# Rotary embedding on one core: longer VectorE operations and stores by even and odd partitions

## Chip, cores and metric

The kernel runs on one core of a Trainium2 chip. The metric is the device time of one execution in microseconds. The times given are medians over several runs; the profile is of one execution, whose own time is given beside it.

## What is computed

The reference applies a rotary position embedding. `x` is float32 of 16 x 512 x 1024; its last dimension is 16 heads of 64. `cos` and `sin` are 512 x 32 and depend on the position in the sequence alone.

```python
x = x.reshape(batch, seq, num_heads, head_dim)
x1, x2 = x[..., :half_dim], x[..., half_dim:]
cos = cos[None, :, None, :]
sin = sin[None, :, None, :]
rotated = np.concatenate([x1 * cos - x2 * sin, x1 * sin + x2 * cos], axis=-1)
```

33.6 MB come in and 33.6 MB go out.

## The kernel before, in words

**Slabs.** The work is cut into eight slabs of 4 MB, 0 to 7. A slab lies on all 128 partitions with eight rows of 1024 elements (8192 float32, 32 KB) on each. Two slabs share a batch of 16 rows a partition, so in DRAM the 32 KB runs of neighbouring partitions of one slab start 64 KB apart (`rows`, L67).

**Room.** One tile, `room` (L58), holds six slots of 32 KB a partition, 0 to 5. The same bytes seen as bf16 are `halves` (L59): twelve half places of 8192 elements, where halves 2k and 2k+1 are the lower and the upper half of slot k. Three tables say where a slab lies: `land[s]` (L62) is the slot that slab s is loaded into, `home[s]` (L63) the half place that holds it as bf16, and `leave[s]` (L64) the slot that it is widened into and stored from.

**Steps of a slab.** A load (L82, issued on SP's queue) brings float32 into its slot. `cast` (L153, ScalarE, L154) writes it as bf16 to its home. `turn` (L162, VectorE) rotates it in place, in two parts of 4096 elements, each of three operations: the slab with the halves of each head swapped, times the sin table, into `turned_part` (in the tile `spare`, L168); the slab times the cos table, in place (L168); the sum of both, in place (L171). `spread` (L157, ScalarE, L158) widens the result to float32 in the slot it leaves from, and a store (L86, SP's queue) writes it out.

**Tables.** The cos and sin rows are loaded by two small DMAs on ScalarE's queue (L105), cast by GpSimd (L137), spread over the partitions by eight matmuls with a selection matrix (L145) and copied to bf16 by VectorE (L150), one table for even and one for odd slabs.

**Order.** From L174 on, the order on ScalarE, VectorE and SP is the order in which the calls are written. SP's queue takes the loads 0 to 5, then 6, then 7 in two pieces, then the stores 0 to 7 (store 1 in two pieces of 4096 elements). A DMA on SP waits until what it needs is done, and those written after it wait behind it. Load 6 goes into a slot that an earlier slab's cast has left, load 7 likewise. `first` (L193), store 0, is made to wait for the larger piece of load 7 (`gate`, L188). The waits between engines and DMAs are put in by the language's tracking of which parts of a tile each instruction reads and writes; they count up semaphores, one for each engine, and eight for the DMAs in turn.

Of the kernel before, what the change touches and what calls it, by code (L numbers as in the profile page):

```python
# [9 lines left out]
@with_exitstack  # L10
def kernel(
    ctx: ExitStack,
    tc: tile.TileContext,
    x: bass.AP,
    cos: bass.AP,
    sin: bass.AP,
    num_heads: int,
    out: bass.AP,
):
    nc = tc.nc  # L20
    P = nc.NUM_PARTITIONS

    batch, seq, dim = x.shape
    nh = num_heads
    hd = dim // nh
    half = hd // 2
    bf16 = mybir.dt.bfloat16
    f32 = mybir.dt.float32

    nb = 2  # L30
    slots = 6
    TAIL = 2
    nslabs = batch // nb
    G = 2
    rpp = nb * seq // P
    W = rpp * dim
    SP = seq // rpp
    TW = rpp * half

    out_flat = out.rearrange("b s h d -> b s (h d)")  # L40

    singles = ctx.enter_context(tc.tile_pool(name="singles", bufs=1))
    psum = ctx.enter_context(tc.tile_pool(
        name="psum", bufs=1, space=bass.MemoryType.PSUM))


    def dram(t, s, k):
        return bass.AP(tensor=t.tensor,
                       offset=t.offset + s // G * (G * nb * seq * dim) + s % G * W,
                       ap=[[G * W, P], [1, k * W]])  # L50


    def view(t, offset, *dims):
        return dataclasses.replace(t, offset=t.offset + offset,
                                   ap=[t.ap[0], *[list(d) for d in dims]])


    room = singles.tile([P, slots * W], f32, tag="room")  # L58
    halves = room.bitcast(bf16)  # L59


    land = (0, 1, 2, 3, 4, 5, 2, 3)  # L62
    home = (0, 1, 2, 3, 8, 9, 0, 1)  # L63
    leave = (5, 2, 5, 1, 2, 4, 5, 0)  # L64


    def rows(t, s, r, n):  # L67
        return bass.AP(
            tensor=t.tensor,
            offset=t.offset + s // G * (G * nb * seq * dim) + s % G * W + r * dim,  # L70
            ap=[[G * W, P], [1, n * dim]])


    def wide(slot, r, n):
        return view(room, slot * W + r * dim, (1, n * dim))


    def thin(s, r, n):
        return view(halves, home[s] * W + r * dim, (1, n * dim))


    def load(s, r, n):  # L82
        return nc.sync.dma_start(out=wide(land[s], r, n), in_=rows(x, s, r, n))


    def store(s, r, n):  # L86
        return nc.sync.dma_start(out=rows(out_flat, s, r, n), in_=wide(leave[s], r, n))

    TR = 32
    TQ = seq // TR // rpp
    TC = seq * half // TR
    spare = singles.tile([P, rpp // 2 * dim // 2], f32, tag="spare")
    turned_part = spare.bitcast(bf16)
    raw = view(spare, 0, (1, TC))
    nc.vector.memset(raw, 0.0)  # L97


    def load_tables(queue):  # L100
        for i, src in enumerate((cos, sin)):
            to = dataclasses.replace(
                raw, offset=raw.offset + i * raw.ap[0][0],
                ap=[[P // TR * raw.ap[0][0], TR], [1, TC]])
            queue.dma_start(out=to, in_=bass.AP(  # L105
                tensor=src.tensor, offset=src.offset, ap=[[TC, TR], [1, TC]]))


    load(0, 0, rpp)
    load_tables(nc.scalar)  # L110
    for s in range(1, slots):
        load(s, 0, rpp)

    GP = SP // G
    GT = G // TQ
    pick = singles.tile([P, 3 * GT * P], bf16, tag="pick")
    nc.gpsimd.memset(pick, 0.0)  # L119


    def selection(g, h):
        return pick[:, (g * GT + h // TQ) * P:(g * GT + h // TQ + 1) * P]


    for g in range(3):
        for h in range(0, G, TQ):
            part = view(selection(g, h), 0, (GP, P // GP), (1, GP))
            nc.gpsimd.affine_select(  # L129
                out=part, in_=part, compare_op=mybir.AluOpType.not_equal,  # L130
                fill=-1.0 if g == 2 else 1.0,
                base=-(1 if g else 0) - h // TQ * (P // TR),
                pattern=[[0, P // GP], [-(G // TQ) * (P // TR), GP]],
                channel_multiplier=1)

    raw_b = singles.tile([P, TC], bf16, tag="raw_b")
    nc.gpsimd.tensor_copy(out=raw_b, in_=raw)  # L137

    tab = {}


    def table(h):
        acc = psum.tile([P, 2 * rpp * hd], f32, tag=f"acc{h}")
        for g, at in ((0, 0), (0, half), (2, rpp * hd), (1, rpp * hd + half)):
            nc.tensor.matmul(  # L145
                view(acc, at, (hd, rpp), (1, half)), selection(g, h),
                view(raw_b, h % TQ * TW, (half, rpp), (1, half)),
                start=True, stop=True)
        tab[h] = singles.tile([P, 2 * rpp * hd], bf16, tag=f"tab{h}", name="tab")
        nc.vector.tensor_copy(out=tab[h], in_=acc)  # L150


    def cast(s, r=0, n=rpp):  # L153
        nc.scalar.copy(out=thin(s, r, n), in_=wide(land[s], r, n))  # L154


    def spread(s, r=0, n=rpp):  # L157
        nc.scalar.copy(out=wide(leave[s], r, n), in_=thin(s, r, n))  # L158
        return store(s, r, n)


    def turn(s):  # L162
        n = rpp // 2
        for r in (0, n):
            low = thin(s, r, n)
            flip = view(low, half, (hd, n * nh), (-half, 2), (1, half))
            for out_, in_, a in ((turned_part, flip, rpp * hd), (low, low, 0)):
                nc.vector.tensor_mul(  # L168
                    out=out_, in0=in_,
                    in1=view(tab[s % G], a + r * hd, (hd, n), (0, nh), (1, hd)))  # L170
            nc.vector.tensor_add(out=low, in0=low, in1=turned_part)  # L171


    with tc.manual_schedule(engines={  # L174
            mybir.EngineType.Activation, mybir.EngineType.DVE, mybir.EngineType.SP}):
        n = rpp // 2
        cast(0, 0, n)
        cast(0, n, n)
        for h in range(G):
            table(h)  # L180
        turn(0)
        cast(1)
        turn(1)
        cast(2)
        load(6, 0, rpp)
        turn(2)
        cast(3)
        gate = load(7, 0, rpp - TAIL)  # L188
        load(7, rpp - TAIL, TAIL)
        turn(3)  # L190
        cast(4)
        cast(5)
        first = spread(0)  # L193
        tc.add_manual_dep(
            first.ins, gate.ins.name,
            mybir.DependencyInfo(mybir.DependencyClass.Sync,
                                 mybir.DependencyReason.DATA),
            reason="behind the loads")
        turn(4)
        cast(6)  # L200
        spread(1, 0, n)
        spread(1, n, n)
        turn(5)
        spread(2)
        spread(3)
        spread(4)
        turn(6)
        cast(7)
        turn(7)
        spread(5)  # L210
        spread(6)
        spread(7)


# [33 lines left out]
```

## Time and profile before

| | us |
|---|---|
| median of 3 runs (161.9 to 162.2) | 162.07 |
| the profiled execution | 162.36 |
| its span, first to last instruction | 160.6 |
| VectorE busy (51 instructions) | 112.8 |
| ScalarE busy (19 instructions) | 113.5 |
| cast of 128x8192, f32 to bf16, mean | 7.018 |
| spread of 128x8192, bf16 to f32, mean | 7.017 |
| VectorE product or sum of 128x4096 bf16, mean | 2.292 |
| a 4 MB store, issue to landing, median | 14.8 |

The profile's page gives busy time of each engine, its busy tenths in 40 slices of the span, the DMA queues (q1 is SP's), and the chain of work that ended last. SP's own waits say what each DMA on SP's queue was held by before it was issued. The timeline lists instructions in order: start, duration, engine, line, operation, output and inputs, and in brackets the idle time before it with what ended it. The trace also keeps, for each DMA, the moment at which each of the 16 DMA engines reported its part landed; "landing" means the last of the 16 unless said otherwise. DMA work overlaps everything else; transfers of one queue are worked off in the order of issue, and one issued while others are under way waits behind them.

### The profile page before, as it was taken

The page shows a single profiled execution, that of the slowest core. Times are in us where ns is not written, and L with a number is a line of the kernel's source. Part 1 is how long each engine was busy: PE and PEld are TensorE (multiplying, and loading weights), DVE is VectorE, ACT ScalarE, POOL GpSimd, SP SyncE. Part 2 cuts the span into 40 slices and gives each one's busy share as a digit, 9 for nine tenths or more (in the row PEclk, how much of TensorE's full clock was granted, in tenths as well). Part 3 has the DMA queues.
Part 4 walks back from the last instruction along what each step waited for, and adds up shares of the span by engine and source line. Part 5 has one row for each costly group of instructions (what it writes and reads, how often), then busy time and mean ns, then how long its engine had stood idle before and what let it go on. Part 6 is the DMA issues. An engine that isn't in the chain of part 4 may idle for free.

```text
span 160.6 us, 195 instructions
## 1 busy us (share of the span) xinstructions
PE 1.9 (1%) x8; PEld 1.1 (1%) x8; DVE 112.8 (70%) x51; ACT 113.5 (71%) x19; POOL 2.1 (1%) x9
## 2 busy tenths in 40 slices
PE   0004000000000000000000000000000000000000
PEld 0002000000000000000000000000000000000000
DVE  1002999999999999999999999999739990000000
ACT  3006949488493966999999799999999999800000
POOL 3001000000000000000000000000000000000000
DMA  7999999999999999999899999999999999999993
GB/s 261 408 408 408 506 392 392 498 416 392 490 424 392 473 441 392 457 392 465 375 506 416 392 441 473 392 433 482 392 433 475 392 416 498 392 392 514 400 392 139
DMA packets 2689, 67.25 MB, mean 419 GB/s; under 512 B 320, under 2 KB 320, under 8 KB 384
## 3 DMA queue, kind: packets, MB, share of 16 engines
q1 hardware_dynamic: 2592, 67.11, 97.4%
q10 hardware_dynamic: 96, 0.13, 0.2%
q14 instruction: 1, 0.01, 0.0%
HBM read 33.69 MB, written 33.55 MB: 419 GB/s over the span
## 4 chain that ended last, share of the span: by engine, by line
DVE 62%; ACT 13%; DMA 7%; issue 3%; PE 1%; POOLq 0%; ACTq 0%; DVEq 0%
DVE room L171 20%; DVE room L168 20%; DVE spare L168 20%; ACT room L158 9%; DMA spare<-in_sin_dram 7%; ACT room L154 4%; DVE tab L150 1%; PE acc L145 1%; POOLq L243 0%; ACTq L105 0%; DVE spare L97 0%; DVEq L168 0%; POOLq L137 0%; ACTq L158 0%
## 5 line engine op out<-in xcount | busy, mean ns | idle before, releaser
L154 ACT CAST room<-room 128x8192 bf16<-128x8192 f32 (+1 forms) x9 | 56.3, 6259 | 22.6 <-DMA room<-in_x_dram 22.5
L158 ACT CAST room<-room 128x8192 f32<-128x8192 bf16 (+1 forms) x9 | 56.0, 6258 | 1.3 <-DMA out_dram<-room 1.0
L168 DVE TENSOR_TENSOR spare<-room,tab 128x4096 bf16<-128x4096 bf16 x16 | 36.7, 2292 | 4.5 <-ACT room L154 3.6
L168 DVE TENSOR_TENSOR room<-room,tab 128x4096 bf16<-128x4096 bf16 x16 | 36.7, 2292 | 0.5
L171 DVE TENSOR_TENSOR room<-room,spare 128x4096 bf16<-128x4096 bf16 x16 | 36.7, 2292 | 0.5
L150 DVE CAST tab<-acc 128x1024 bf16<-128x1024 f32 x2 | 2.4, 1220 | 13.6 <-PE acc L145 13.6
L154 ACT ACT_TABLE_LOAD x1 | 1.3, 1283 | 2.6 <-issue 2.6
L145 PE MATMUL acc<-raw_b,pick 128*128 128x256 bf16 x8 | 1.9, 416 | 13.9 <-POOL raw_b L137 13.9
L145 PEld LDWEIGHTS <-pick 128*128 128x128 bf16 x8 | 1.1, 139 | 14.2 <-issue 12.2
L97 DVE MEMSET spare<- 128x512 f32 x1 | 0.5, 485 | 0.9 <-PEq L229 0.9
L129 POOL TENSOR_SCALAR_AFFINE_SELECT pick<-pick 128x128 bf16<-128x128 bf16 x3 | 0.8, 308 | 0.1
L137 POOL CAST raw_b<-spare 128x512 bf16<-128x512 f32 x1 | 0.6, 610 | 11.2 <-DMA spare<-in_sin_dram 11.2
L119 POOL MEMSET pick<- 128x384 bf16 x1 | 0.4, 417 | 0.3 <-POOLq L229 0.3
L229 POOL MEMSET const-bfloat16-1.0<- 128x1 bf16 x1 | 0.1, 101 | 0.0
L229 POOL MEMSET const-uint8-127<- 128x1 uint8 x1 | 0.1, 101 | 0.0
L229 POOL MEMSET const-float32-0.0<- 128x1 f32 x1 | 0.1, 98 | 0.2 <-issue 0.2
L229 POOL MEMSET const-float32-1.0<- 128x1 f32 x1 | 0.1, 98 | 0.0
## 6 DMA issues: line engine op xcount, KB each, us to landing
room<-in_x_dram SPq DMA_DIRECT2D x7, 4096.0 KB, 31.7
out_dram<-room SPq DMA_DIRECT2D x7, 4096.0 KB, 14.8
out_dram<-room SPq DMA_DIRECT2D x2, 2048.0 KB, 9.9
room<-in_x_dram SPq DMA_DIRECT2D x1, 3072.0 KB, 29.4
room<-in_x_dram SPq DMA_DIRECT2D x1, 1024.0 KB, 31.5
spare<-in_cos_dram ACTq DMA_DIRECT2D x1, 64.0 KB, 7.9
spare<-in_sin_dram ACTq DMA_DIRECT2D x1, 64.0 KB, 11.1
```

What stands on the lines that cost most here:

```text
L97: nc.vector.memset(raw, 0.0)
L119: nc.gpsimd.memset(pick, 0.0)
L129: nc.gpsimd.affine_select(out=part, in_=part, compare_op=mybir.AluOpType.not_equal, fill=-1.0 if g == 2 else 1.0, base=-(1 if g else 0) - ...
L137: nc.gpsimd.tensor_copy(out=raw_b, in_=raw)
L145: nc.tensor.matmul(view(acc, at, (hd, rpp), (1, half)), selection(g, h), view(raw_b, h % TQ * TW, (half, rpp), (1, half)), start=True, sto ...
L150: nc.vector.tensor_copy(out=tab[h], in_=acc)
L154: nc.scalar.copy(out=thin(s, r, n), in_=wide(land[s], r, n))
L158: nc.scalar.copy(out=wide(leave[s], r, n), in_=thin(s, r, n))
L168: nc.vector.tensor_mul(out=out_, in0=in_, in1=view(tab[s % G], a + r * hd, (hd, n), (0, nh), (1, hd)))
L171: nc.vector.tensor_add(out=low, in0=low, in1=turned_part)
L229: nc = _bacc.Bacc("TRN2", target_bir_lowering=False, num_devices=1)
```

## The change

Five parts.

- Slabs 0, 1, 2, 5 and 7 (`aside`) are rotated in three operations of 8192 elements instead of six of 4096. The products with sin go into a half place that is free at the time instead of `turned_part`. Slabs 3, 4 and 6 are rotated as before.
- Slabs 6 and 7 change landing slots (6 into slot 3, 7 into slot 2), and slabs 1 and 4 leave from slot 3 instead of slot 2.
- Load 5 is issued after turn(0) is written, not among the first loads, since the sin products of slab 0 lie in slot 5.
- Slab 0 is cast in one operation instead of two, cast(3) is written ahead of load 6 and turn(2), and turn(3) behind cast(5).
- The stores of slabs 2 to 5 are two DMAs each (`twice`): the even partitions, then the odd ones, 64 rows of 32 KB in each.

```diff
-    land = (0, 1, 2, 3, 4, 5, 2, 3)
+    land = (0, 1, 2, 3, 4, 5, 3, 2)
     home = (0, 1, 2, 3, 8, 9, 0, 1)
-    leave = (5, 2, 5, 1, 2, 4, 5, 0)
+    aside = {0: 10, 1: 3, 2: 4, 5: 1, 7: 4}
+    leave = (5, 3, 5, 1, 3, 4, 5, 0)
...
+    def every_other(t, i):
+        (step, count), rest = t.ap[0], t.ap[1:]
+        return dataclasses.replace(t, offset=t.offset + i * step,
+                                   ap=[[2 * step, count // 2], *rest])
+
+
+    def twice(s, r=0, n=rpp):
+        for i in (0, 1):
+            nc.sync.dma_start(out=every_other(rows(out_flat, s, r, n), i),
+                              in_=every_other(wide(leave[s], r, n), i))
...
-    for s in range(1, slots):
+    for s in range(1, slots - 1):
         load(s, 0, rpp)
...
     def turn(s):
-        n = rpp // 2
-        for r in (0, n):
+        n = rpp if s in aside else rpp // 2
+        for r in range(0, rpp, n):
             low = thin(s, r, n)
             flip = view(low, half, (hd, n * nh), (-half, 2), (1, half))
-            for out_, in_, a in ((turned_part, flip, rpp * hd), (low, low, 0)):
+            crossed = (view(halves, aside[s] * W, (1, n * dim))
+                       if s in aside else turned_part)
+            for out_, in_, a in ((crossed, flip, rpp * hd), (low, low, 0)):
                 nc.vector.tensor_mul(
                     out=out_, in0=in_,
                     in1=view(tab[s % G], a + r * hd, (hd, n), (0, nh), (1, hd)))
-            nc.vector.tensor_add(out=low, in0=low, in1=turned_part)
+            nc.vector.tensor_add(out=low, in0=low, in1=crossed)
...
-        cast(0, 0, n)
-        cast(0, n, n)
         for h in range(G):
             table(h)
+        cast(0)
         turn(0)
+        load(5, 0, rpp)
         cast(1)
         turn(1)
         cast(2)
+        cast(3)
         load(6, 0, rpp)
         turn(2)
-        cast(3)
         gate = load(7, 0, rpp - TAIL)
         load(7, rpp - TAIL, TAIL)
-        turn(3)
         cast(4)
         cast(5)
-        first = spread(0)
+        turn(3)
+        spread(0)
+        first = store(0, 0, rpp)
...
         turn(4)
         cast(6)
-        spread(1, 0, n)
-        spread(1, n, n)
+        for r in (0, n):
+            spread(1, r, n)
+            store(1, r, n)
         turn(5)
-        spread(2)
-        spread(3)
-        spread(4)
+        for s in (2, 3, 4):
+            spread(s)
+            twice(s)
         turn(6)
         cast(7)
         turn(7)
-        spread(5)
-        spread(6)
-        spread(7)
+        for s in (5, 6, 7):
+            spread(s)
+            (twice if s == 5 else store)(s, 0, rpp)
```

In the changed program the cast stands at L167, the spread at L171, the products at L182, the sum at L185, the loads at L84, the plain stores at L88 and the stores by even and odd partitions at L99.

More of the change, by code (lines that the diff above doesn't have):

```diff
@@ L158, in spread @@
         nc.scalar.copy(out=wide(leave[s], r, n), in_=thin(s, r, n))
-        return store(s, r, n)
     def turn(s):
-        n = rpp // 2
-        for r in (0, n):
+        n = rpp if s in aside else rpp // 2
+        for r in range(0, rpp, n):
             low = thin(s, r, n)
             flip = view(low, half, (hd, n * nh), (-half, 2), (1, half))
-            for out_, in_, a in ((turned_part, flip, rpp * hd), (low, low, 0)):
+            crossed = (view(halves, aside[s] * W, (1, n * dim))
+                       if s in aside else turned_part)
+            for out_, in_, a in ((crossed, flip, rpp * hd), (low, low, 0)):
                 nc.vector.tensor_mul(
```

## The prediction

> **What bounds the kernel now.** I read the page first, then SP's own waits, then the timeline, then the trace's landing records. The page:
>
> ```profile
> span 160.6 us, 195 instructions
> ...
> DMA  7999999999999999999899999999999999999993
> ...
> q1 hardware_dynamic: 2592, 67.11, 97.4%
> q14 instruction: 1, 0.01, 0.0%
> ...
> DVE 62%; ACT 13%; DMA 7%; issue 3%; PE 1%; POOLq 0%; ACTq 0%; DVEq 0%
> ```
>
> The DMA row is full from the second slice to the last but one, and queue q1's packets take 97.4% of what 16 engines have. The chain of waits names DVE at 62%, but it follows releasers between compute engines. The same trace shows that store 7 was only the last of a queue:
>
> ```profile
> SPq L87 <- ACT room L158: 58.1, 8, 13.5
> ...
> SPq L243 <- DMA out_dram<-room: 19.2, 1, 19.2
> ```
>
> SP issues store 7 at 139.96 and then waits 19.2 us for it to land; 4 MB alone takes about half of that. The landing records give the rate: loads 1 to 5 land at 22.81, 32.52, 42.23, 51.95 and 61.66 (9.71 apart), stores 2 and 3 at 110.21 and 119.88 (9.67 apart). No gap lies between them, so the engines stream 16 transfers of 4 MB end to end, and the end is load 0's start plus 16 transfers. VectorE and ScalarE matter only where a store is issued after the queue has run dry. Around the change the timeline reads:
>
> ```profile
> 90.97 20.99 ACT L158 CAST room<-room 128x8192 f32<-128x8192 bf16 x3 [0.97 <-DMA out_dram<-room]
> ...
> 111.86 7.01 ACT L154 CAST room<-room 128x8192 bf16<-128x8192 f32 x1
> ...
> 118.91 2.29 DVE L168 TENSOR_TENSOR spare<-room,tab 128x4096 bf16<-128x4096 bf16 x1 [3.57 <-ACT room L154]
> ...
> 132.92 7.02 ACT L158 CAST room<-room 128x8192 f32<-128x8192 bf16 x1 [0.20 <-DVE room L171]
> ```
>
> These are spreads 2 to 4 (issuing stores 2, 3, 4 at 98.01, 105.06, 111.99), cast(7), slab 7's first product, and spread(7). The slack is small: store 1's second half lands at 95.7 to 100.55 and store 2 is issued at 98.01, 2.5 us ahead; store 5 is issued at 125.83, while store 4 lands at 129.5 (one engine 130.53), 3.7 us ahead.
>
> **The change, part by part.** Times below continue this trace.
>
> *Three operations of 8192.* One product of 4096 takes 2.292 us, 2.325 from start to start. None of 8192 is in the trace. Above: two of 4096, 4.58. Below: two less a whole fixed cost, which is at most the 0.485 us of the 128x512 memset: 4.10. ScalarE's same doubling went 3.604 to 7.018, 0.19 under twice; I take that row's step: 4.39, 4.43 with the gap, 13.3 us a slab against 13.95. Nothing is gained by it while the queue is full, as VectorE waits for ScalarE and ScalarE for DMA.
>
> *Start.* cast(0) as one operation runs 13.29 to 20.31 (7.02); turn(0) ends at 33.65, turn(1) at 46.9, turn(2) at 60.2. The free half places make new true waits: load 5 waits for turn(0) (33.65; its turn in the queue comes at 51.95), cast(3) for turn(1) (46.9 to 53.9, 4.6 us later than now), load 6 for cast(3) (53.9; turn at 61.66), load 7 for turn(2) (60.2; turn at 71.38). Each is issued 7 to 18 us before the queue needs it: cost nothing. If the cover went, each would cost at most a restart, 2.8 us below. Behind load 5 on SP stand only the loads just timed. turn(3) ends at 74.2, turn(4) at 88.2; spread(0) is at 68.8 as now, and store 0 still waits for load 7's landing at 78.7. turn(5) now waits for spread(1) (90.0), since its products lie where slab 1 was: 90.03 to 103.3.
>
> *Stores as even and odd partitions.* SP gets four more DMAs of 0.33 us each, hidden in its waits. Store 1 already goes in two pieces, and these land 4.83 us after each other, half of 9.67, so the splitting alone costs nothing. What costs is in the waits that the built program gives the instructions around these stores. In the changed program:
>
> ```
> ACT 17 L167 TensorCopy room<-room 128x8192 [waits DMAHW3_49,DMAHW2_49,DMAHW6_49,DMAHW1_49,DMAHW7_49,DMAHW0_49,DVE_49]
> DVE 28 L182 TensorTensor room<-room,tab 128x4096 [waits DMAHW3_49,DMAHW2_49,DMAHW6_49,DMAHW1_49,DMAHW7_49,DMAHW0_49,DVE_49]
> SP 9 L99 DMACopy out_dram<-room 64x8192 [waits DMAHW6_49,DVE_49,Activation_49]
> SP 15 L99 DMACopy out_dram<-room 64x8192 [waits DMAHW4_49,DVE_49,Activation_49]
> ```
>
> The eight DMA semaphores go round in the order of issue; by their counts the first row, cast(7), waits for the full landing of both halves of stores 2, 3 and 4. So does the second, the second product of turn(6). Both write slot 0, and stores 2, 3 and 4 read slots 5, 1 and 3: no data is shared, yet the waits are there, and with plain stores in the same places the built program has none of them. By the counts of DVE, store 2 also waits for turn(5)'s last operation and store 5 for turn(7)'s.
>
> Now the sum. Store 2 is ready at 98.0, but goes at turn(5)'s end, 103.35. The queue is dry at 100.55. A restart is in the trace once: load 0 is issued at 0.73 and lands at 13.27, 12.54 us, 2.83 over a queued load. Its bounds are 1.0 (issue to first packet at 1.74) and 2.83; I take 2.83, the one whole row. Stores 2, 3 and 4 then land by 103.35 + 2.83 + 3 x 9.67 = 135.2. (Spreads 3 and 4 are done at 105.1 and 112.1, ahead of need.)
>
> At 135.2 two things start. cast(7) runs to 142.2. VectorE has five operations of turn(6) left, 5 x 2.325 = 11.6, to 146.85, then turn(7), 13.3, to 160.15. Queued behind cast(7) on ScalarE are spread(5) (142.2 to 149.2) and spread(6) (to 156.3); neither helps, as SP waits for turn(7) before store 5 and takes stores in order. Store 5 goes at 160.2, into engines idle since 135; store 6 follows at once and store 7 when spread(7) is done (160.2 + 7.0 = 167.2, long before the queue reaches it). The last landing is 160.2 + 2.83 + 3 x 9.67 = 192.0. Now it is 159.49 in a span of 160.6, so 1.1 follows: span 193.1. The profiled execution took 162.36, 1.8 over its span: **194.9**. The median of the runs shown, 162.07, is 0.3 less: 194.6, which I round to **194.5**.
>
> **The rivals.**
>
> *A. The stores of 64 partitions run at half rate.* Every engine moves a 32 KB row in 1.213 us, all 16 at once. If even rows are dealt so that two engines share a path, stores 2 to 5 take 19.34 each: 4 x 9.67 = 38.7 more, **233**. For it: no transfer of x or out in the trace has a partition step of two. Against: the two table loads, 32 rows on every fourth partition, have landing records from 16 engines each, and 64 rows divide as well. [...]
>
> *B. They run somewhat slower.* Each row in DRAM now lies 128 KB from the next instead of 64 KB. At 10 to 30% on 38.7 us the end moves by 4 to 12: **198 to 206**. Stores with the present pitch run at 9.67 against 9.71 for loads, so the pitch has not hurt so far. [...]
>
> *C. The waits cost nothing, and the time is not longer.* This needs their counts to be reached by earlier transfers on the same semaphores, before ScalarE comes to cast(7) at 112. Then cast(7), turn(7) and store 5 stay where they are, the queue never dries, and only the tail changes. In the last store 15 engines land by 158.66 and one at 159.49. That one falls behind between stores 3 and 4, where the single 8 KB packet of q14 (instructions) runs at 120.9, as VectorE enters its last slab. With 15 VectorE operations fewer that fetch may not come inside the span: 162.36 - 0.83 = **161.5**, otherwise 162.4. The deciding point is the count: the wait on DMAHW3 is for 48, three transfers of 16, and load 1 and store 0 make only 32; the third is store 4's odd half. I see no way around it.
>
> **How the numbers follow.** Forecast 0.66, A 0.14, B 0.14, C 0.04, and 0.02 for something slower that I have not thought of. The forecast's own bounds: restarts of 1.0 instead of 2.83 take off 3.7, products of 4.10 another 1.7, giving 189.1; products of 4.58 add 1.1, giving 195.6. With B on top the range is 189 to 207 and leaves out A, C and the rest. A measurement of this kernel tells about 0.2% from no change. Faster comes from C alone, 0.03, with 0.01 for no difference; slower 0.96.
>
> **What would show it.** The DMA row should have a shallow dip near 101 to 105 and a hole of some 26 us from about 135, then a full stretch of 30 us. cast(7) should start behind a wait of about 23 us (112 to 135) for out's DMA, and VectorE should idle from about 105.6, inside turn(6), until the same moment. SP's wait before store 5 should end with a VectorE operation of turn(7). If the hole is there but stores 2 to 4 land 58 us after their start, A holds. If cast(7) starts near 112, the reading of the waits is wrong, and with it the whole forecast. If each restart is nearer to 1 us, I am up to 4 us too high.

## The result and the profile after

The changed kernel takes 193.13 us (median of 5, 193.08 to 193.21), the one before 162.07: 1.192 times as long, 95% interval 1.190 to 1.193. The profiled execution took 193.21, with a span of 191.4. The forecast was 194.5 in a range of 189 to 207.

The page of the changed kernel, with the rows that were shown of the one before, and those of VectorE and ScalarE:

```profile
span 191.4 us, 181 instructions
...
DVE  1004799999999999995999000000899993000000
ACT  2019494931998999998999940000899956800000
...
DMA  6999999999999999999982999989000005999995
...
q1 hardware_dynamic: 2656, 67.11, 81.9%
```

The same bytes took 81.9% of a longer span. The DMA row now has a dip (the digits 8 and 2, 96 to 105 us) and five empty slices (134 to 158); a slice is 4.8 us. VectorE's row has its six empty slices before that, 105 to 134, while the DMA engines are busy: the two take turns. The row of q14, the instruction packet, is gone. In the kernel before, VectorE's row had no such hole:

```profile
DVE  1002999999999999999999999999739990000000
```

Who waited for whom, in the same kernel (total, times, longest):

```profile
DVE room L182 <- DMA out_dram<-room: 29.1, 1, 29.1
ACT room L167 <- DMA out_dram<-room: 22.7, 1, 22.7
```

SP's own waits:

```profile
SPq L99 <- DVE room L185: 58.7, 2, 45.7
```

And the timeline around the hole:

```profile
103.45 2.28 DVE L182 TENSOR_TENSOR spare<-room,tab 128x4096 bf16<-128x4096 bf16 x1
103.59 57.28 SPq L99 DMA_DIRECT2D out_dram<-room  x8
134.79 7.02 ACT L167 CAST room<-room 128x8192 bf16<-128x8192 f32 x1 [22.69 <-DMA out_dram<-room]
134.85 2.29 DVE L182 TENSOR_TENSOR room<-room,tab 128x4096 bf16<-128x4096 bf16 x1 [29.12 <-DMA out_dram<-room]
...
155.27 4.42 DVE L185 TENSOR_TENSOR room<-room 128x8192 bf16<-128x8192 bf16 x1
159.79 7.02 ACT L171 CAST room<-room 128x8192 f32<-128x8192 bf16 x1 [4.14 <-DVE room L185]
160.97 6.20 SPq L88 DMA_DIRECT2D out_dram<-room  x2
```

cast(7), which ran at 111.86 before, waits 22.7 us for a store to land and runs at 134.79; the second product of turn(6) waits 29.1 us until the same moment. The last half of store 4 lands at 134.53. SP's first row counts two waits for VectorE: store 2 until turn(5) ends and, the longest, store 5 from 114 until turn(7) ends at 159.7. By the landing records store 5's first half lands at 166.3 and store 7 at 190.59.

### The profile page after: what moved, and what is told of

The parts are those of the page before. It is cut to its first block, busy times and chain, and to the rows that moved or that the text cites. A ratio compares the mean times of both kernels' runs of the same rounds, so it can differ in the third digit from the quotient of the medians.

```text
span 191.4 us, 181 instructions
## 1 busy us (share of the span) xinstructions
PE 1.9 (1%) x8; PEld 1.1 (1%) x8; DVE 110.0 (57%) x36; ACT 113.3 (59%) x18; POOL 2.1 (1%) x9
## 3 DMA queue, kind: packets, MB, share of 16 engines
q1 hardware_dynamic: 2656, 67.11, 81.9%
## 4 chain that ended last, share of the span: by engine, by line
DMA 34%; DVE 29%; ACT 16%; issue 7%; SPq 0%; DVEq 0%; ACTq 0%
DVE room L182 21%; DMA out_dram<-room 18%; DMA room<-in_x_dram 16%; ACT room L171 12%; DVE room L185 7%; ACT room L167 4%; DVE spare L182 1%; SPq L99 0%; DVEq L182 0%; ACTq L171 0%; SPq L88 0%
## 5 line engine op out<-in xcount | busy, mean ns | idle before, releaser
L167 ACT CAST room<-room 128x8192 bf16<-128x8192 f32 x8 | 56.0, 7018 | 45.7 <-DMA out_dram<-room 22.7
L182 DVE TENSOR_TENSOR room<-room,tab 128x8192 bf16<-128x8192 bf16 (+1 forms) x16 | 58.0, 3624 | 34.5 <-DMA out_dram<-room 29.1
L171 ACT CAST room<-room 128x8192 f32<-128x8192 bf16 (+1 forms) x9 | 56.0, 6258 | 5.2 <-DVE room L185 4.1
L185 DVE TENSOR_TENSOR room<-room 128x8192 bf16<-128x8192 bf16 x5 | 22.1, 4425 | 0.2
L185 DVE TENSOR_TENSOR room<-room,spare 128x4096 bf16<-128x4096 bf16 x6 | 13.8, 2292 | 0.2
L182 DVE TENSOR_TENSOR spare<-room,tab 128x4096 bf16<-128x4096 bf16 x6 | 13.7, 2289 | 0.2
## 6 DMA issues: line engine op xcount, KB each, us to landing
out_dram<-room SPq DMA_DIRECT2D x3, 4096.0 KB, 19.9
```

The lines of the kernel that those rows point to most:

```text
L182: nc.vector.tensor_mul(out=out_, in0=in_, in1=view(tab[s % G], a + r * hd, (hd, n), (0, nh), (1, hd)))
L185: nc.vector.tensor_add(out=low, in0=low, in1=crossed)
```

## The experiments

Two theories stood against each other. W: the stores with a partition step of two make the program wait where no data is shared, and these waits are the whole loss. L: the longer operations, the borrowed places and the later loads cost it. S, beside them: moving 64 alternate partitions is slow by itself.

### Plain stores, all else as changed (`plain`)

```diff
         for s in (2, 3, 4):
             spread(s)
-            twice(s)
+            store(s, 0, rpp)
...
-            (twice if s == 5 else store)(s, 0, rpp)
+            store(s, 0, rpp)
```

> The changed kernel with plain stores of 128 partitions for slabs 2 to 5; all else as changed. Theory W (the waits that the stores with a partition step of two bring in cost everything): store 2 is issued at 98, cast(7) starts at 112, the queue never dries, 161.3 us if the instruction fetch of the last slab is gone as well, 162.1 if not. Rival L (the longer operations, the new places and the later loads cost it): 170 to 193, with the hole near 135 still there.

161.52 us (161.43 to 161.83), 0.9967 of the kernel before, interval 0.9954 to 0.9979. W holds and L falls: with every longer operation, borrowed place and later load in, the kernel is a little faster than before. Its page and timeline:

```profile
DMA  7999999999999999999999999999999999999994
...
q1 hardware_dynamic: 2592, 67.11, 97.9%
```

```profile
111.94 7.01 ACT L167 CAST room<-room 128x8192 bf16<-128x8192 f32 x1
...
118.99 8.88 DVE L182 TENSOR_TENSOR room<-room,tab 128x8192 bf16<-128x8192 bf16 x2 [1.68 <-ACT room L167]
```

cast(7) is back at 111.94, 0.08 from where it was before, and the queue never dries.

### Even and odd stores, one tile for each slot (`tiles`)

```diff
-    room = singles.tile([P, slots * W], f32, tag="room")
-    halves = room.bitcast(bf16)
+    slot_tiles = [singles.tile([P, W], f32, tag=f"room{k}", name="room") for k in range(slots)]
+    half_tiles = [t.bitcast(bf16) for t in slot_tiles]
+
+    def place(h, r, n):
+        return view(half_tiles[h // 2], h % 2 * W + r * dim, (1, n * dim))
```

The rest of the edit, not shown, lets `wide`, `thin` and the sin products take their place from these tiles.

> The changed kernel with its even and odd stores, but six tiles of one slot each instead of one tile of six slots, same bytes and same order. Theory W: the stores and the writes to slot 0 are now in different tiles, so the waits go and the time is that of plain stores, 161.2 to 162.1 us. Rival S (transfers of 64 alternate partitions cost time by themselves): at least 1 us over the kernel with plain stores; 200 if they ran at half rate.

161.49 us (161.28 to 161.54), 0.9956, interval 0.9945 to 0.9968: as with plain stores. The transfers are those of the changed kernel, eight DMAs of 64 rows with a partition step of two; only the tiles that hold the slots differ. Its DMA row is full again:

```profile
DMA  7999999999999999999999999999999999999995
```

By the landing records the eight halves land 4.83 to 4.84 us apart, half of the 9.67 of a whole store. So S falls, and with it rivals A and B of the prediction. In its trace cast(7) starts at 111.94 and turn(6) runs through without a gap; no wait for a store is left but the 0.9 us before spread(2), which were there before the change as well.

### The kernel before, with even and odd stores and nothing else (`before_twice`)

```diff
...
         nc.scalar.copy(out=wide(leave[s], r, n), in_=thin(s, r, n))
-        return store(s, r, n)
+        return (twice if 2 <= s <= 5 else store)(s, r, n)
```

The lines left out define `every_other` and `twice` as in the changed kernel.

> The kernel before, with nothing but the stores of slabs 2 to 5 as even and odd partitions. Theory W: store 2 waits for turn(5) (101.4), stores 2 to 4 land by 132.4, cast(7) and the rest of turn(6) wait for that, turn(7) ends at 158.3, store 7 lands at 189.2: 191.8 us. Rival L: the old operations and places bring the time back to 162 or 163.

191.78 us (191.75 to 191.86). The old operations and places bring nothing back. Its waits are the ones of the changed kernel:

```profile
DVE room L180 <- DMA out_dram<-room: 28.9, 1, 28.9
ACT room L166 <- DMA room<-in_x_dram: 22.6, 6, 9.5
ACT room L166 <- DMA out_dram<-room: 20.6, 1, 20.6
```

The first and third row are the hole; the second, the casts of the first slabs waiting for their loads, was there before the change as well. The split of the stores makes the loss by itself, in either kernel.

### The waits one by one (`only5`, `only234`)

Even and odd partitions for store 5 alone, then for stores 2, 3 and 4 alone, each in the changed kernel.

> The changed kernel with even and odd partitions for store 5 alone. Theory W: store 5 waits for turn(7)'s end, 132.4 instead of 125.9; the queue is dry from 129.6; from the changed kernel's restart (159.76 to 190.59, 30.8 us for three stores) the last landing is 163.2 and the time 165.9. Rival (that wait is covered): 161.5.

166.09 us (166.06 to 166.63). SP's row of this run is store 5 held by turn(7):

```profile
SPq L99 <- DVE room L185: 19.9, 1, 19.9
```

The 19.9 us are not the price: SP could not have used the first 13.5, since spread(5) ends at 125.8, and of the rest the queue covers all but the gap from 129.5 to the issue at 132.33 and one restart. The price is 166.09 - 161.52 = 4.6.

> The changed kernel with even and odd partitions for stores 2, 3 and 4, and store 5 plain. Theory W: the hole near 135 opens as before, but store 5 goes when spread(5) is done, 148.75, not after turn(7), 159.8; last landing 148.75 + 30.8 = 179.6, time 182.2. Rival (the hole is the wait of store 5, not of cast(7)): 166 or less.

181.85 us (181.80 to 181.92). The hole is there, but store 5 is issued at spread(5)'s end:

```profile
148.63 18.41 SPq L88 DMA_DIRECT2D out_dram<-room  x3
155.15 4.42 DVE L185 TENSOR_TENSOR room<-room 128x8192 bf16<-128x8192 bf16 x1
```

The two do not add up: alone they cost 4.6 and 20.3, together 31.6, because the wait for turn(7) is for the most part covered by the queue in the one case, while in the other it stands behind the hole: store 5 goes at 159.76 instead of 148.63.

### Halves of neighbouring partitions (`lowhigh`)

```diff
-        return dataclasses.replace(t, offset=t.offset + i * step,
-                                   ap=[[2 * step, count // 2], *rest])
+        return dataclasses.replace(t, offset=t.offset + i * step * (count // 2),
+                                   ap=[[step, count // 2], *rest])
```

> The changed kernel with its split stores as partitions 0 to 63 and then 64 to 127, instead of even and odd; still one tile. The built program has none of the waits of cast(7), turn(6) and store 2, and store 5 waits for turn(5) alone. Theory W (the waits come from the partition step of two, not from splitting): 161.3 to 162 if half the partitions still move at full rate. Rival P (64 neighbouring partitions move at half rate): each 2 MB piece takes 9.67 instead of 4.83 us, 38.7 us more, 200; the hole near 135 is absent in either case. [...]

199.34 us; its four runs scatter from 197.07 to 200.63, and the profile is of the longest, so only the size of it is used. The waits of cast(7) and turn(6) are gone (cast(7) starts at 111.91), in one tile and with the stores split, so it is the step of two that brings them. The time is lost in another way. Columns: stretch, its length, five engines' busy time, clock, DMA share, GB/s.

```profile
80.00:90.00 10.00, 0.00 (x0) 0.00 (x0) 7.99 (x4) 9.97 (x3) 0.00 (x0) 1.00 1.01 437
...
104.00:114.00 10.00, 0.00 (x0) 0.00 (x0) 9.86 (x5) 10.00 (x3) 0.00 (x0) 1.00 1.04 226
114.00:124.00 10.00, 0.00 (x0) 0.00 (x0) 8.25 (x4) 10.00 (x2) 0.00 (x0) 1.00 1.00 223
```

Whole transfers, in the first row, move 437 GB/s, the halves of neighbouring partitions 223 to 226, with the DMA engines busy all the time; a row of 32 KB takes 2.55 us instead of 1.21 (medians). In the three windows after these, to 154, it is 239 to 265 GB/s. This is the half rate that rival A feared, in the split that the change did not choose. What makes neighbouring partitions slow no run here shows.

### The last 0.6 us (`plain_pad`, `plain_pad30`, `plain_pad8`)

Plain stores are 0.55 us faster than the kernel before. Theory F: VectorE's instruction fetch makes one DMA engine late before, and with fewer VectorE instructions it does not come. First, 16 small memsets at the start of the kernel:

```diff
+    for k in range(16):
+        nc.vector.memset(singles.tile([P, 1], f32, tag=f"pad{k}", name="pad"), 0.0)
```

> The kernel with plain stores, with 16 memsets of one element a partition put first on VectorE, so that VectorE has about as many instructions as before. Theory F (the instruction fetch of VectorE makes one DMA engine late): an 8 KB packet of q14 comes back inside the span, one engine lands some 0.8 us after the other 15, and the time is 0.6 to 0.9 us over plain, near 162.1. Rival: the time is that of plain within 0.2, whatever made the engine late before.

162.02 us, the time that F expected, but no packet of q14 in the span (one comes at 160.7, behind the last instruction), so the number is luck and does not bear F out. The 16 DMA engines end 0.66 us apart instead of 0.43, and from the last landing to the end of the span it is 0.4 us longer; these memsets also delay the two table loads by 0.45 us. Why it is slower stays open. So the memsets were moved behind the tables, where VectorE waits anyway:

```diff
         for h in range(G):
             table(h)
+        for k in range(30):
+            nc.vector.memset(singles.tile([P, 1], f32, tag=f"pad{k}", name="pad"), 0.0)
```

> Plain stores, with 30 memsets of one element a partition on VectorE behind the tables, where it waits for cast(0) anyway; VectorE then has 11 instructions more than in the kernel before. Theory F (the instruction fetch makes one DMA engine late): the 8 KB packet of q14 is inside the span while stores run, one engine lands about 0.8 us behind the others from there on, 162.1 to 162.4. Rival: within 0.2 of plain stores, 161.5.

162.20 us, interval of the ratio 0.9996 to 1.0016: the gain is gone. The packet is back, at 78.1 us:

```profile
q14 instruction: 1, 0.01, 0.0%
```

By the landing records one engine then finishes load 7's larger piece at 79.60, the other 15 by 78.89, and it is still 0.42 us behind them at the end. To part the fetch from the padding, three kernels ran on one chip:

> Plain stores once more, on the same chip as the two kernels with padding, so that these can be set beside it: 161.5.

> Plain stores with 8 memsets of one element a partition on VectorE behind the tables: more instructions, but too few to reach the fetch. Theory F (the instruction fetch costs, not the padding): no packet of q14, the 16 engines together at the end, and the time within 0.2 of plain stores. Rival (instructions on VectorE cost by themselves, or their places do): a good quarter of what 30 memsets cost, 161.7 or more.

> The 30 memsets once more, on the same chip. Theory F: the packet of q14 in the span, one engine 0.4 to 0.8 us late at the end, 0.4 to 0.9 us over plain stores.

161.59, 161.60 and 162.18 us; ratios to before 0.9972 (0.9961 to 0.9984), 0.9971 (0.9962 to 0.9981) and 1.0008 (0.9999 to 1.0016). Eight more VectorE instructions cost nothing; thirty bring the packet back, one engine lands 0.44 us behind the rest, and 0.6 us go. F holds for these and for the kernel before, whose late engine fell behind 0.98 us just as its packet ran at 120.9. In the trace's packet records each row of a DMA engine starts as the one before it ends (beside the packet to within 3 ns), so the packet can be placed: on its engine the 32 KB row ahead of the packet takes 1.516 us, the packet 0.309 and the row behind it 1.571, where a row takes 1.213; together they explain 0.97 us. In `before_twice` the packet runs at 145.9, in the hole, and all 16 engines land store 7 within 0.2 us. For 16 memsets F does not explain the time.

## Why the prediction was right

*The waits.* The step that carried the forecast was that cast(7) and the second product of turn(6) wait for the landing of store 4, and store 5 for turn(7). Each is in the trace within a microsecond of the times worked out: store 2 issued at 103.6 (103.35), cast(7) at 134.8 (135.2), store 5 at 159.8 (160.2). Taking the waits away in two ways gave 161.5 both times, and adding them to the old kernel gave 191.8.

*The restart was mis-sized.* The prediction took 2.83 us, load 0's excess over a queued load. Store 2's issue at 103.59 to store 4's landing at 134.53 is 30.94, less 3 x 9.67 = 29.01, leaves 1.93; from store 5's issue at 159.76 to store 7's landing is 30.83, which leaves 1.82. Two restarts were 1.9 us too dear together, more than the whole error of 1.4 in the last landing; store 2, issued 0.24 late, and the 0.3 named below took the rest back. Load 0 was the wrong row: it is a load, at the kernel's start, and this excess was measured between stores. Why load 0's is larger, no run here shows.

*Small terms.* The operation of 8192 takes 4.425 us (4.39 taken), but from its first start to its last end turn(7) takes 13.33, as worked out (13.3). From the landing of store 4 to the first instruction it is 0.26 us on ScalarE and 0.32 on VectorE, which had not been counted. A split store takes SP 0.47 to 1.39 us to issue, not 0.33; this stayed hidden. From the last landing to the end of the span it is 0.83, not 1.1.

*What was costed at nothing* cost nothing: load 5 was issued at 33.9, load 6 at 54.2 and load 7 at 60.4, and `plain`, which has them all, is not slower.

*The rivals.* A and B fell with `tiles`, the pitch of 128 KB that B feared included. No run shows the shared path that A supposes, nor the 10 to 30% of B that the range's 207 holds: with even and odd stores the halves land 4.83 to 4.84 us apart, half of 9.67. C named the mechanism that would have made the change faster, and its 161.5 is what the kernel gives when the waits are taken out; it was not the likelier one, since the count on the semaphore could not be reached without store 4.

Not settled: why cast(7) and turn(6), which write slot 0, wait for stores from slots 5, 1 and 3 with a partition step of two (22.7 and 29.1 us), and why the one from slot 5 waits for turn(5)'s last operation, which writes slot 4. The runs show only that the step brings the waits in one tile (cast(7) at 134.79), and that neither one tile per slot (111.94) nor a step of one (111.91) has them.

## What to carry to other kernels

Where the DMA queue is full, look at what each instruction waits for in the built program before costing an edit: here an access pattern that moves the same bytes in another order brought waits of 22.7 and 29.1 us for stores that share no data with the waiting instructions, and these put the engines and the queue in turns instead of side by side (193.1 us against 161.5). Two waits can cost more behind each other than the sum of what each costs alone (4.6 and 20.3 us here, 31.6 together). The version to keep is the one with plain stores, or one tile per slot: 161.5 us, 0.3 to 0.4% under the kernel before.

## What the runs showed of the hardware that was not expected

- With plain stores, 30 memsets and a single 8 KB instruction packet among 67 MB the kernel takes 162.2 us; with 8 memsets or none, and no packet, 161.6. The packet runs 0.3 us, but what its DMA engine moves beside it is drawn out too (in the kernel before, rows of 1.516 and 1.571 us instead of 1.213): that engine falls 0.7 to 1.0 us behind the other 15 and makes up 0.15 to 0.3 of it before the end. `plain_pad` is the exception: 162.02 with no packet in the span.
- The same 64 partitions' worth of bytes moves at 433 GB/s as every other partition (`tiles`, 2.1 MB in 4.84 us) and at first at about 225 GB/s as neighbours (`lowhigh`, 104 to 124 us).
